# First FFN of a hybrid SSD/Hyena layer: gate and up products by seven block products, hidden values through DRAM, down product as a pass of its own

## The chip, the cores and the metric

The kernel runs on one core of a Trainium2 chip. The metric is the time of one execution on the device in microseconds (us), lower is better. The time before is the median of three runs.

## What is computed

One inference step of a layer over 1280 tokens: 1024 latent tokens (shift, scale and gate from `c`) and 256 context tokens (from `c_ctx`). The model width is 1024, the FFN width 2752, and all arithmetic is to float32 accuracy. Cut to what matters here:

```python
def swiglu(h, w_gate, w_up, w_down):
    return jnp.dot(jax.nn.silu(jnp.dot(h, w_gate)) * jnp.dot(h, w_up), w_down)

def trunk_layer(x, cond, ssd_init, n_rows, p):
    mod = jnp.dot(jax.nn.silu(cond), p['w_ada']) + p['b_ada']
    sh1, sc1, g1, sh2, sc2, g2, sh3, sc3, g3 = jnp.split(mod[:, None, :], N_MOD, axis=-1)
    h = modulate(rmsnorm(x, p['norm_ffn1']), sh1, sc1)
    x = x + 0.5 * g1 * swiglu(h, p['ffn1_w_gate'], p['ffn1_w_up'], p['ffn1_w_down'])
    h = modulate(rmsnorm(x, p['norm_mix']), sh2, sc2)
    mix, final_state = token_mix(h, ssd_init, n_rows, p)
    x = x + g2 * mix
    h = modulate(rmsnorm(x, p['norm_ffn2']), sh3, sc3)
    x = x + 0.5 * g3 * swiglu(h, p['ffn2_w_gate'], p['ffn2_w_up'], p['ffn2_w_down'])
    return x, final_state
```

A final RMSNorm follows. The change is in the first `swiglu` and in what stands directly before and behind it.

## The kernel before

**Precision.** Every float32 operand of a large product is split into a high part, rounded for TensorE, and a low part, the rest: `split` has a cast on ScalarE (line 137) and a subtraction on VectorE (138). `mm3` (lines 629 to 633) then issues three matmuls, high by high, high by low and low by high. A 128x128 weight block against a tile of tokens is so three matmuls, one of each of lines 631, 632 and 633.

**Stages.** In order of time: a front stage (`filters`: the Hyena filters and their spectra, with the first 16 adaLN units and the first norm woven in), the first FFN, the mixer, the output product, the second FFN with the final norm.

**First FFN before** (`ffn`, from line 647). The FFN width is 21 full units of 128 and a half unit of 64 (`NFULL` = 21). Tokens are in groups of 512, 512 and 256. Units go in slabs of two: gate and up of both units for all three groups (tile `pg`, 8 blocks of the model width each), then the down product of the slab (tile `pd`), which VectorE adds into x, which stays in SBUF (line 701). After each slab `hook` runs some of the 56 remaining adaLN units. The closing slab goes by a table (`PLAN1`), in which groups are finished in the order 2, 0, 1 and their norm for the mixer is woven into the rest.

**An adaLN unit** (`mod_unit`) is one 512 KB load (`wa`) and two multiply-and-sum instructions of 128x1024 on VectorE (`junk`, line 173), with a few very short ones.

**Second FFN before**, the scheme that the change copies. `products` (line 341) takes the tokens in two halves of 640 (`HT`; matmuls are 320 wide, `HB`) and the model width in two halves of 4 blocks. For each full unit gate and up weights are a 2x2 block matrix and tokens another, and seven block products (`P1` to `P7`) stand in for eight:

```python
"P1": (p("A11", "B11", "z", "pp1"), ...), "P6": (p("S2", "T2", "w", "pp6"), ...),
"P2": (p("A12", "B21", "z"), ...),        "P7": (p("S3", "T3", "x", "pp7"), ...),
"P5": (p("S1", "T1", "y", "pp5"), ...),   "P4": (p("A22", "T4", "x"), ...), "P3": (p("S4", "B22", "y"), ...)
```

One block product is 2 token strips x 4 blocks x 3 matmuls = 24 matmuls of 320 columns. `T1` to `T4` are differences of weight blocks (VectorE); `S1` to `S4` are sums of the modulated token halves, made once by `halves_s`: per k two operations on VectorE (514, 516) and two on GpSimd (515, 517), then `cut` splits each (S2's high parts are among the tiles `yp`, its low parts are `S2l`). The half unit 21 takes four plain products (`pt`). The list `ramp` of products that need no sums comes first (six items in the second FFN). The results leave PSUM by ScalarE copies and VectorE additions (`e1` to `e7`), and the hidden values go to DRAM. `strassen` (481) prepares weights four items ahead. Then `down_steps` (520) goes over the token groups one after the other: per step one unit's hidden values (`hraw`, split into `hs`) and its down weights (`wd`, split into `dh` and `dl`), two steps ahead, 8 x 3 matmuls into 8 PSUM banks; x is loaded again from DRAM and the eviction adds it. Weights of nine units are kept in split form after the first pass, the others are loaded and split again for each group.

**Order of work.** Each engine takes its instructions in the order in which a scheduler puts them for that engine when the kernel is built; semaphores are the only coupling. All loads here are issued by SyncE (SP), in order too. Tile pools with few buffers make a load wait for the last reader of the buffer that it fills.

Of the kernel before, what the change touches and what calls it, by code (L numbers as in the profile page):

```python
# [18 lines left out]
D = 1024  # L19
# [91 lines left out]
class Kern:  # L111
# [7 lines left out]
    def setup(self):  # L119
# [11 lines left out]
        self.wn = 0  # L131
        self.silu = None
# [176 lines left out]
    def rstd_half(self, x, tp, pp, ptag, dst):  # L309
# [13 lines left out]
        def mm():  # L323
            st["ps"] = pp.tile([128, 2, 512], F32, name="nps", tag=ptag)[:, :, :HB]
            for b in range(2):
                nc.tensor.matmul(st["ps"][:, b, :], self.ones, st["acc"][:, HB * b:HB * b + HB], start=True, stop=True)
# [14 lines left out]
    def products(self, wgu, hidd, S, wp, tt, ee, pp, raws, ramp, hook=None):  # L341
# [14 lines left out]
        def tsum(name, j, a, b):  # L356
            if (j, name) not in made:
                t = made[j, name] = tt.tile([128, 512], F32, name=name, tag=name)
                nc.vector.tensor_tensor(out=t, in0=a, in1=b, op=ALU.subtract)
            return made[j, name]  # L360
# [9 lines left out]
            "V2": lambda j: tsum("t2", j, half_raw(1, 1), half_raw(1, 0)),  # L370
        }

        def half_raw(half, k):
            if ("t", half, k) not in made:
                t = made["t", half, k] = tt.tile([128, 512], F32, name=f"wt{half}{k}", tag=("t1", "t3")[k])
                nc.sync.dma_start(t, wgu[2 * NFULL][:, 512 * k:512 * k + 512])
            return made["t", half, k]
# [30 lines left out]
        def pair(j):  # L408
# [27 lines left out]
            def e4():  # L436
                c = et("c21", "c21")
# [41 lines left out]
        return [(prep(j, c), f, e, load(j, c)) for j, (f, c, e) in seq]  # L479
# [47 lines left out]
    def down_steps(self, wdn, hidd, xsrc, mg, order, js, keep, at, each, pre, tick=None):  # L527
# [70 lines left out]
        def loadx(g, dm):  # L598
            g0, gw, _ = GROUPS[g]
            x[g, dm] = at(None)["x"].tile([128, 512], F32, name="xr", tag="x")[:, :gw]  # L600
# [168 lines left out]
    def win_zdt(self, h, zd, wz, rz, tp, pp, ptag):  # L769
        nc = self.nc  # L770
        w = [[self.wsplit(self.i["wz"][half, q], width=WUNIT, pool=wz, rp=rz) for q in range(2)] for half in range(2)]
# [424 lines left out]
    def filter_lat(self, o, hbig, w3, dl, ctn, caf, cb, tp, kp, pp, ptag):  # L1196
# [29 lines left out]
        def spec(bk):  # L1226
# [18 lines left out]
            def s3():  # L1245
                kk = kp.tile([128, T], F32, name="fk", tag="h")
                k = kk[:, 0:512]
                nc.scalar.copy(k, r["pz"])
                if bk == 0:
                    q = kk[64:65, 512:1024]  # L1250
# [338 lines left out]
    def build(self):  # L1589
# [13 lines left out]
        hp0 = sb("hp0")  # L1603
        h0 = self.hpool(hp0, "h", (0,))
        xp, hd, tp, modp = sb("xp", side="right"), sb("hd", 4, "right"), sb("tp", 2, "right"), sb("modp", side="right")
        nr = sb("nr", side="right")
        x = tiles(xp, "x")

        def load_x():
            for k in range(KD):  # L1610
                nc.sync.dma_start(x[k], i["xT"][k])
        mods = [(lambda u=u: self.mod_unit(u, modp)) for u in range(16)]
        np1 = sb("np1", 3, "right")
        r1 = []
# [3 lines left out]
        np1.release()  # L1618
        hp1, pp = sb("hp1"), psum("pp", 4)
        h = pair({**h0, **self.hpool(hp1, "h", (1, 2))})  # L1620
        self.wp = sb("wp", 6)
        self.wb = sb("wb", 4)
        fs = self.norm_items(x, 0, h, 2, TagPool(pp, "dn"), pp, "gu", tp)
# [355 lines left out]
```

## Time and profile before

| what | us |
|---|---|
| median of 3 runs (2673.14 to 2676.66) | 2673.55 |
| the profiled execution's own time | 2677.57 |
| its span in the trace | 2675.8 |
| TensorE (PE) busy | 2602.1 (97%) |
| VectorE (DVE) busy | 1519.8 (57%) |
| ScalarE (ACT) busy | 964.9 (36%) |
| GpSimd (POOL) busy | 16.6 (1%) |
| mean granted TensorE clock, share of full | 0.991 |

The profile is of one execution. PE's busy time is the union of its matmuls' records; records overlap, so the pace is read from start to start. A line number is a line of the kernel before. In the trace's rows a tile is named without its number (`pp1` is `pp`), a weight load is PEld, and "[4.03 <-ACT yp L137]" behind an instruction says that its engine sat idle for 4.03 us before it and which instruction ended that.

### The profile page before, as it was taken

How to read it: one execution, taken by the hardware profiler on the slowest of the kernel's cores; microseconds unless marked ns; L12 is line 12 of the kernel's file. 1: busy time of each engine (PE TensorE's matmuls, PEld its weight loads, DVE VectorE, ACT ScalarE, POOL GpSimd, SP SyncE). 2: the span in 40 equal slices, each digit the busy share in tenths (PEclk: the TensorE clock that was granted, in tenths of full speed). 3: DMA queues.
4: the chain of work that ended last, by engine and by line, in shares of the span. 5: the costliest groups of instructions: out<-in, count | busy, mean ns of one | idle time of the engine just before them, and what ended most of it. 6: DMA issues, size and time to landing. Idle time of an engine off the chain costs nothing.

```text
span 2675.8 us, 37129 instructions
## 1 busy us (share of the span) xinstructions
PE 2602.1 (97%) x14843; PEld 2268.5 (85%) x14843; DVE 1519.8 (57%) x2584; ACT 964.9 (36%) x1689; POOL 16.6 (1%) x15
## 2 busy tenths in 40 slices
PE   7999999999999999999999898997999999999998
PEld 3668888888888888798778787997999999988888
DVE  7677545655456336815885457569545545542445
ACT  4772111111111114623784676445222222232233
POOL 0000000000000000000000000002000000000000
PEclk9999999999999999999999999998999999999999
DMA  7433222222222112211224434631222222263334
GB/s 259 141 112 109 87 79 79 80 71 72 78 79 86 41 32 87 94 52 52 73 67 154 144 120 141 213 121 58 71 76 78 66 63 78 65 219 116 127 126 151
DMA packets 127184, 268.68 MB, mean 100 GB/s; under 512 B 14423, under 2 KB 50079, under 8 KB 126627
## 3 DMA queue, kind: packets, MB, share of 16 engines
q1 hardware_dynamic: 127011, 266.31, 31.2%
q8 instruction: 116, 1.90, 0.3%
q14 instruction: 57, 0.47, 0.1%
HBM read 211.53 MB, written 54.73 MB: 100 GB/s over the span
## 4 chain that ended last, share of the span: by engine, by line
PE 88%; DVE 5%; ACT 3%; DMA 2%; issue 1%; SPq 0%; POOL 0%; DVEq 0%; ACTq 0%; POOLq 0%
PE pg L631 7%; PE pg L633 7%; PE pg L632 7%; PE pd L631 7%; PE pd L633 7%; PE pd L632 7%; PE pp L632 6%; PE pp L633 6%; PE pp L631 6%; PE pc L631 3%; PE pc L632 3%; PE pc L633 3%; PE po L632 1%; PE po L633 1%; PE po L631 1%
## 5 line engine op out<-in xcount | busy, mean ns | idle before, releaser
L631 PE MATMUL pg<-hh,wh 128*128 128x512 f32 (+1 forms) x1032 | 366.2, 355 | 2.0 <-ACT wh L137 2.0
L633 PE MATMUL pg<-hh,wl 128*128 128x512 f32 (+1 forms) x1032 | 365.6, 355 | 0.0
L632 PE MATMUL pg<-hl,wh 128*128 128x512 f32 (+1 forms) x1032 | 365.4, 355 | 0.0
L631 PEld LDWEIGHTS pg<-hh,wh 128*128 128x128 f32 x1032 | 195.3, 189 | 30.4 <-ACT wh L137 3.3
L633 PEld LDWEIGHTS pg<-hh,wl 128*128 128x128 f32 x1032 | 195.4, 189 | 27.4 <-DVE wl L138 0.4
L632 PEld LDWEIGHTS pg<-hl,wh 128*128 128x128 f32 x1032 | 195.3, 189 | 27.1
L631 PE MATMUL pp<-yp,wT 128*128 128x320 f32 x672 | 209.6, 312 | 8.9 <-ACT yp L137 8.8
L633 PE MATMUL pp<-yp,wT 128*128 128x320 f32 x672 | 209.4, 312 | 0.0
L701 DVE SCALAR_TENSOR_TENSOR x<-pd,mod,x 128x512 f32<-128x512 f32 (+1 forms) x264 | 167.4, 657 | 51.1 <-PE pd L633 46.8
L173 DVE CUSTOM_DVE_ANT_0 junk<-wa,scb 128x1024 bf16<-128x1024 f32 x144 | 175.5, 1219 | 36.2 <-DMA wa<-wada 35.3
L138 DVE TENSOR_TENSOR wl<-wr,wh 128x1024 fp32r<-128x1024 f32 (+1 forms) x103 | 125.3, 1224 | 114.2 <-ACT wh L137 113.5
L631 PE MATMUL pd<-hh,wh 128*128 128x512 f32 (+1 forms) x504 | 182.1, 361 | 0.5 <-DVE x L701 0.5
L633 PE MATMUL pd<-hh,wl 128*128 128x512 f32 (+1 forms) x504 | 179.7, 357 | 0.0
L632 PE MATMUL pd<-hl,wh 128*128 128x512 f32 (+1 forms) x504 | 179.3, 356 | 0.0
L631 PE MATMUL pd<-hs,dh 128*128 128x512 f32 (+1 forms) x504 | 177.5, 355 | 1.0 <-DVE nm L220 0.8
L632 PE MATMUL pd<-hs,dh 128*128 128x512 f32 (+1 forms) x504 | 178.1, 354 | 0.1
L633 PE MATMUL pd<-hs,dl 128*128 128x512 f32 (+1 forms) x504 | 177.5, 354 | 0.0
L137 ACT CAST wh<-wr 128x1024 fp32r<-128x1024 f32 (+1 forms) x103 | 107.1, 1048 | 174.5 <-PE pd L632 52.9
L673 ACT ACTIVATE ft<-pg 128x512 f32<-128x512 f32 (+1 forms) x66 | 34.6, 524 | 354.9 <-PE pg L633 354.8
L631 PE MATMUL pc<-hh,wh 128*128 128x512 f32 (+1 forms) x432 | 154.8, 360 | 1.5 <-ACT hh L239 1.5
L631 PE MATMUL pp<-sh,wB 128*128 128x320 f32 x504 | 156.1, 310 | 0.0
L633 PE MATMUL pp<-sh,wB 128*128 128x320 f32 x504 | 155.6, 309 | 0.0
(381 smaller groups left out, 5819.8 us busy)
## 6 DMA issues: line engine op xcount, KB each, us to landing
wa<-wada SPq DMA_DIRECT2D x72, 512.0 KB, 3.6
wd<-wdn SPq DMA_DIRECT2D x45, 512.0 KB, 3.3
wr<-wgu SPq DMA_DIRECT2D x43, 512.0 KB, 3.5
wg<-wgu SPq DMA_DIRECT2D x42, 512.0 KB, 3.6
wr<-wdn SPq DMA_DIRECT2D x21, 512.0 KB, 3.5
hraw<-hidd SPq DMA_DIRECT2D x42, 256.0 KB, 2.6
wr<-wc SPq DMA_DIRECT2D x18, 512.0 KB, 3.6
kd<-fk SPq DMA_DIRECT2D x32, 256.0 KB, 2.4
```

What stands on the lines that cost most here:

```text
L137: nc.scalar.copy(hi, src)
L138: nc.vector.tensor_tensor(out=lo, in0=src, in1=hi.bitcast(F32), op=ALU.subtract)
L173: nc.vector.tensor_tensor_reduce(out=junk, in0=w, in1=self.scb[cond], scale=1.0, scalar=0.0, op0=ALU.mult, op1=ALU.add, accum_out=self.mod ...
L631: nc.tensor.matmul(ps, wh, rh, start=first, stop=False, **more)
L632: nc.tensor.matmul(ps, wh, rl, start=False, stop=False, **more)
L633: nc.tensor.matmul(ps, wl, rh, start=False, stop=last, **more)
L673: self.silu = nc.scalar.activation(t, pg, AF.Silu)
L701: nc.vector.scalar_tensor_tensor(out=x[dm][:, sl], in0=ps[dm], scalar=self.mod[:, mg, dm, cond:cond + 1], in1=x[dm][:, sl], op0=ALU.mult, ...
```

## The change

The first FFN takes the scheme of the second. In detail:

- `ffn` is no longer called. `products` and `down_steps` run for the first FFN as well, with hidden values in `hida`, token halves from a new input `xP` (x with each half's tokens side by side) and `ramp` of four items. Matmuls of 320 columns, 21 x 7 x 24 + 4 x 24 = 3624 of them, take the place of 3096 of 512 and 256; the down product keeps its number and widths.
- Front stage: `norms0` normalizes and modulates both halves (16 tiles, each two VectorE and two ScalarE instructions, of 512 and 128 columns) and splits half 0. Before, it was the norm of group 0 with its 8 modulated, split tiles and the root of group 1; the rest of the norm ran inside the first FFN.
- Down pass of the first FFN: groups in the order 0, 1, 2. Only units 2 to 5 keep their split weights, and these are given up at step 3 of the third pass, when the buffers of group 2's mixer input are made.
- adaLN units: one with each item of `B11` and `B21` from item 9 on (two in a unit's seven items, 40 in all), through a single buffer (`mw`), the next load issued behind the unit; 16 more in steps 1 to 16 of the first down pass, also through one buffer.
- Handover to the mixer: group 2's norm comes last, other order of the first mixer units.
- Shared helpers (so the second FFN too): `T1` is split right behind `T2` and not at its own product; `tt` is one tag of two buffers; tile `c21` comes from another pool; `rstd_half` writes two single PSUM banks and reads them by two instructions. `win_zdt` loses a raw buffer of its own; the filters' tile `fk` is 512 wide.

The core of the diff:

```diff
+    def mod_load(self, u, pool):
+        self.mraw[u] = pool.tile([128, D], F32, name=f"wa{u}", tag="wr")
+        self.nc.sync.dma_start(self.mraw[u], self.i["wada"][u])
+
     def mod_unit(self, u, pool):
...
-        w = self.raw(f"wa{u}")
-        nc.sync.dma_start(w, self.i["wada"][u])
+        if u not in self.mraw:
+            self.mod_load(u, self.rp)
+        w = self.mraw.pop(u)
...
@@ rstd_half @@
-            nc.vector.tensor_scalar(out=v2(m), in0=st["ps"], scalar1=1.0 / D, scalar2=EPS, op0=ALU.mult, op1=ALU.add)
+            for b, ps in enumerate(st["ps"]):
+                nc.vector.tensor_scalar(out=m[:, HB * b:HB * b + HB], in0=ps, scalar1=1.0 / D, scalar2=EPS, op0=ALU.mult,
+                                        op1=ALU.add)
...
@@ products @@
-                t = made[j, name] = tt.tile([128, 512], F32, name=name, tag=name)
+                t = made[j, name] = tt.tile([128, 512], F32, name=name, tag="t")
...
+        order = [(j, c) for j, (_, c, _) in seq]
+        for j in range(NFULL):
+            order.remove((j, "T1"))
+            order.insert(order.index((j, "T2")) + 1, (j, "T1"))
+        return [(prep(*order[n]), f, e, load(*order[n]), c) for n, (j, (f, c, e)) in enumerate(seq)]
...
@@ the program @@
-        self.filters(sb, psum, hd, lambda: self.mod_begin(modp), one(mods), lambda pp, ptag: one(
-            self.norm_items(x, 0, pair(h0), 0, np1, pp, ptag) +
-            self.rstd_items(x, 1, r1, np1, pp, ptag, dst=nr.tile([128, 512], F32, name="r1"))), load_x)
+        def norms0(pp, ptag):
+            banks = lambda: [pp.tile([128, 512], F32, name="nps", tag=ptag)[:, :HB] for _ in range(2)]
+
+            def mod(half, k):
+                self.modulate(xa[half][k], rr[half], 0, k)
+                if half == 0:
+                    self.split(xa[0][k], a1[0][k], a1[1][k])
+            out = []
+            for half in range(2):
+                out += self.rstd_half(xa[half], np1, banks, lambda half=half: rr[half])
+                out += [lambda half=half, k=k: mod(half, k) for k in range(KD)]
+            return one(out)
+        self.filters(sb, psum, hd, lambda: self.mod_begin(modp), one(mods), norms0, load_x)
...
+        sbp, mw = sb("sbp", 5, "right"), sb("mw", 1, "right")
+        sums, cut = self.halves_s(S, xa, xp, a1, yt, sbp)
+        items = self.products(i["wgu1"], hidd, S, self.wp, tt, ee, xp, pp, [self.rp] * 2,
+                              [(0, "P1"), (0, "P2"), (NFULL, None), (NFULL, None)])
...
+        def mods1(pool):
+            self.mod_unit(units.pop(0), modp)
+            if units:
+                self.mod_load(units[0], pool)
+
+        def more(s):
+            if s < 2:
+                for k in (2 * s, 2 * s + 1):
+                    sums(k)
+                    cut("S2", k)
+            elif s < 6:
+                for k in range(4):
+                    cut(("S3", "S1", "A22", "S4")[s - 2], k)
+            elif s > 8 and items[s][4] in ("B11", "B21"):
+                mods1(mw)
...
+        def tick(p, q):
+            if p and 2 <= q < 2 + KD:
+                norms[p - 1][KD - 1 + q]()
+            if p == 0 and q and units:
+                mods1(pl["mw"])
+            if p == 2 and q == 3:
+                pl["keep"].release()
+                ps = pl["h2"], pl["xg"], pl["np", 2] = sb("hp2"), sb("xg", 8), sb("xn", 4)
...
+        load, split, step, n = self.down_steps(i["wdn1"], hidd, i["xT"], 2, (0, 1, 2), [range(NFULL + 1), rest, rest],
+                                               range(2, 6), at, each, lambda p: norms[p - 1][KD](), tick)
+        self.strassen(items, 4, more, {len(items) - 1: prologue})
...
-        tail = self.ffn(i["wgu1"], i["wdn1"], h, x, 2, hd, tp, pp, after, hook, begin, (2, 0, 1), PLAN1, turn)
...
-        pipe([un[j][2] for j in range(3)])
-        run(tail[:KD])
-        pipe([un[0][0], un[1][0]])
-        run(tail[KD:KD + 1])
-        pipe([un[2][0]])
-        run(tail[KD + 1:])
+        pipe([un[0][0]])
+        run(norms[2][KD:KD + 1])
+        pipe([un[1][0], un[2][0]])
+        run(norms[2][KD + 1:])
+        pipe([un[j][1] for j in range(3)])
```

**Three places in the order of instructions.** The first is ScalarE at the end of the front stage. There `fut` and `fk` are the copies of the filters' spectra, `hh` is a modulated high part for the first FFN, `xa_117` to `xa_119` are modulated tiles of half 1. Before:

```order
165 L1248 COPY fk<-pfz 128x512
166 L1239 COPY fut<-pft 128x512
167 L192 ACTIVATE nr<-nm 128x512
168 L1248 COPY fk<-pfz 128x512
169 L193 ACTIVATE nr<-nr 128x512
170 L1248 COPY fk<-pfz 128x512
171 L137 CAST wh_1423<-wr_1421 128x1024
```

With the change:

```order
186 L347 ACTIVATE xa_117<-xa_117,mod 128x128
187 L1262 COPY fk<-pfz 128x512
188 L1254 COPY fut<-pft 128x512
189 L347 ACTIVATE xa_118<-xa_118,mod 128x512
190 L347 ACTIVATE xa_118<-xa_118,mod 128x128
191 L1262 COPY fk<-pfz 128x512
192 L1254 COPY fut<-pft 128x512
193 L347 ACTIVATE xa_119<-xa_119,mod 128x512
```

Between two spectra's copies there now stand two modulations of half 1; before, the last copies had only the reciprocal root between them.

The second is VectorE where the first FFN begins. Before, it made the weights' low parts (`wl`) and the modulated tokens of group 1:

```order
210 L138 TENSOR_TENSOR wl_1428<-wr_1427,wh_1429 128x1024
211 L237 SCALAR_TENSOR_TENSOR nt<-x_121,msc,r_374 128x512
212 L237 SCALAR_TENSOR_TENSOR nt<-x_122,msc,r_374 128x512
213 L237 SCALAR_TENSOR_TENSOR nt<-x_123,msc,r_374 128x512
214 L240 SCALAR_TENSOR_TENSOR hl_0_1391<-nt,mod,hh_0_1383 128x512
```

Now (`t` is a difference of weight blocks, `sf` and `xa` are sums of token halves, `S2l` a low part of S2, `wa` an adaLN row):

```order
246 L367 TENSOR_TENSOR t_1534<-wg_1_1528,wg_0_1513 128x512
247 L531 TENSOR_TENSOR xa_105<-sf_1481,xa_105 128x640
248 L367 TENSOR_TENSOR t_1536<-wg_1_1528,t_1534 128x512
249 L182 TENSOR_SCALAR mod<-mod,pkt 128x2
250 L179 ISA junk,mod<-wa_1933,scb_255 128x1024
251 L179 ISA mod 128x1
252 L139 TENSOR_TENSOR wT_0_1533<-t_1536,wT_0_1533 128x512
253 L139 TENSOR_TENSOR S2l_1571<-xa_105,sy_1465 128x640
254 L529 TENSOR_TENSOR sf_1482<-xa_114,xa_118 128x640
```

The sums stand between weight splits and halves of adaLN units; the modulations are all ahead of them.

The third is VectorE in the first down pass. Before, adaLN units stood in the first FFN between the splits of the hidden values (`hl`):

```order
365 L674 TENSOR_TENSOR ft<-ft,pg 128x512
366 L138 TENSOR_TENSOR hl_2139<-ft,hh_2138 128x512
367 L173 ISA junk,mod<-wa_2531,scb_248 128x1024
368 L173 ISA mod 128x1
```

Now a step's splits and one unit alternate:

```order
937 L139 TENSOR_TENSOR dl_7261<-wd_7215,dh_7262 128x1024
938 L139 TENSOR_TENSOR hs_7265<-hraw,hs_7265 128x512
939 L179 ISA junk,mod<-wa_7211,scb_255 128x1024
940 L179 ISA mod 128x1
941 L179 ISA junk,mod<-wa_7211,scb_258 128x1024
942 L179 ISA mod 128x1
943 L182 TENSOR_SCALAR mod<-mod,pkt 128x2
944 L139 TENSOR_TENSOR dl_7305<-wd_7259,dh_7306 128x1024
```

The splits for a later step (`dl_7305`) stand behind a unit whose row comes through the one buffer.

## Rows read from the trace of the kernel before

**Rows 1.** Page, part 4: the chain that ended last, shares of the span by engine.

```profile
PE 88%; DVE 5%; ACT 3%; DMA 2%; issue 1%; SPq 0%; POOL 0%; DVEq 0%; ACTq 0%; POOLq 0%
```

**Rows 2.** Busy time by windows; columns: window, length, engines (instructions), PEclk, DMA share, GB/s.

```profile
111.00:168.00 57.00, 52.89 (x260) 33.08 (x258) 34.70 (x58) 49.71 (x90) 0.00 (x0) 1.00 0.33 107
143.00:168.00 25.00, 23.22 (x98) 12.78 (x98) 11.14 (x17) 24.67 (x49) 0.00 (x0) 1.00 0.44 147
235.00:1030.00 795.00, 795.00 (x4165) 682.64 (x4163) 409.82 (x678) 119.41 (x178) 0.00 (x0) 1.00 0.23 72
1840.00:1845.00 5.00, 0.95 (x4) 0.55 (x3) 2.78 (x5) 3.93 (x7) 2.75 (x2) 0.50 0.37 102
1850.00:2275.00 425.00, 424.94 (x2884) 424.68 (x2882) 229.50 (x328) 108.11 (x174) 0.00 (x0) 1.00 0.24 72
2640.00:2654.00 14.00, 14.00 (x119) 14.00 (x118) 6.67 (x10) 5.98 (x9) 0.00 (x0) 1.00 0.64 207
```

**Rows 3.** PE by tile (pg, pd, pp): count, ns min/median/max, first and last start.

```profile
L631 PE MATMUL pg<-hh,wh x1032: 277/389/796, 169.1 to 1061.4; 128*128 128x512 f32 x127, 128*128 128x256 f32 x45
L694 PE MATMUL pd<-hs,wl x24: 278/392/402, 1015.9 to 1072.9; 128*128 128x512 f32 x16, 128*128 128x256 f32 x8
L631 PE MATMUL pp<-sh,wB x504: 304/309/556, 1805.4 to 2358.9; 128*128 128x320 f32 x168
L631 PE MATMUL pd<-hs,dh x504: 278/389/800, 2359.4 to 2659.9; 128*128 128x512 f32 x112, 128*128 128x256 f32 x56
L589 PE MATMUL pd<-hs,dl x24: 279/389/390, 2474.4 to 2662.0; 128*128 128x512 f32 x16, 128*128 128x256 f32 x8
```

**Rows 4.** Timeline of PE; start, duration. 27 steps lie between the first two, 26 between the last.

```profile
599.77 0.39 PE L631 MATMUL pg<-hh,wh 128*128 128x512 f32 x1
...
605.89 0.39 PE L631 MATMUL pg<-hh,wh 128*128 128x512 f32 x1
...
1999.69 0.31 PE L632 MATMUL pp<-S3l,wT 128*128 128x320 f32 x1
...
2003.52 0.31 PE L631 MATMUL pp<-yp,wT 128*128 128x320 f32 x1
```

**Rows 5.** Timeline of PE: the two longest idle times at the second FFN's start.

```profile
1834.76 0.64 PE L631 MATMUL pp<-yp,wT 128*128 128x320 f32 x1 [4.03 <-ACT yp L137]
...
1844.91 0.64 PE L631 MATMUL pp<-yp,wT 128*128 128x320 f32 x1 [4.05 <-ACT yp L137]
```

**Rows 6.** Groups at the second FFN's start, 1815 to 1850 us: busy us, mean ns, idle before.

```profile
L337 DVE SCALAR_TENSOR_TENSOR xa<-xa,msc,nr 128x512 f32<-128x512 f32 x8 | 11.2, 1396 | 0.0
...
L515 POOL TENSOR_TENSOR xa<-xa,xa 128x640 f32<-128x640 f32 x4 | 7.4, 1870 | 1825.5 <-DVE sf L514 1825.5
...
L516 DVE TENSOR_TENSOR xa<-sf,xa 128x640 f32<-128x640 f32 x4 | 4.5, 1152 | 1.4 <-POOL xa L515 1.4
...
L138 DVE TENSOR_TENSOR wT<-t,wT 128x512 fp32r<-128x512 f32 x4 | 2.7, 683 | 0.1
```

**Rows 7.** Groups on ACT: `hh` from 111 to 168.1 us, the others from 1690 to 1850 us.

```profile
L239 ACT ACTIVATE hh<-nt,mod 128x512 fp32r<-128x512 f32 x8 | 5.8, 721 | 0.2
...
L339 ACT ACTIVATE xa<-xa,mod 128x512 f32<-128x512 f32 x16 | 11.6, 723 | 5.4 <-DVE xa L337 5.4
...
L137 ACT CAST sh<-xa 128x640 fp32r<-128x640 f32 x12 | 8.4, 725 | 0.2
...
L339 ACT ACTIVATE xa<-xa,mod 128x128 f32<-128x128 f32 x16 | 6.3, 394 | 1.9 <-DVE xa L337 1.9
```

**Rows 8.** Page, parts 5 and 6: adaLN units; the last column is issue to landing, us.

```profile
L173 DVE CUSTOM_DVE_ANT_0 junk<-wa,scb 128x1024 bf16<-128x1024 f32 x144 | 175.5, 1219 | 36.2 <-DMA wa<-wada 35.3
...
wa<-wada SPq DMA_DIRECT2D x72, 512.0 KB, 3.6
```

**Rows 9.** Timeline of PE: idle times between the first FFN and the mixer.

```profile
1094.63 1.12 PE L217 MATMUL nps<-nacc,ones 128*128 128x512 f32 x2 [1.45 <-DVE nacc L212]
...
1102.50 0.98 PE L631 MATMUL pc<-hh,wh 128*128 128x512 f32 x3 [1.48 <-ACT hh L239]
```

More of the change, by code (lines that the diff above doesn't have):

```diff
@@ new lines, in build, with late, tile, each @@
+        pl, norms, h = {}, {}, [{}, {}]
+        at = lambda s: {"raw": (self.rp, D, "wr"), "hid": (self.wp, "w")} if s is not None and s < 2 else pl
+        def late(g):
+            class Late:
+                def tile(_, shape, dtype, name, tag):
+                    return pl["psum"].tile(shape, dtype, name=name, tag="b" if g == 2 else "dn")
+            return Late()
+        def each(g, dm, x):
+            g0, gw, _ = GROUPS[g]
+            nc.sync.dma_start(xd[dm][:, g0:g0 + gw], x[g, dm])
+            if dm == 0:
+                norms[g] = self.norm_items(lambda k: x[g, k], 1, h, g, pl["np", g], late(g), "dn")
+            else:
+                norms[g][dm - 1]()
+            if dm == KD - 1:
+                norms[g][dm]()
@@ new lines, in tick @@
+        def tick(p, q):
[6 more added lines that the diff above has]
+                ps = pl["h2"], pl["xg"], pl["np", 2] = sb("hp2"), sb("xg", 8), sb("xn", 4)
+                for n in range(2):
+                    h[n][2] = [ps[0].tile([128, 256], F32R, name=f"h2{n}{k}") for k in range(KD)]
+        rest = [2, 3, 4, 5, 0, 1, *range(6, NFULL + 1)]
@@ new lines, in build @@
+        hp0, hp1, kp = sb("hp0"), sb("hp1"), sb("kp1", 8)
+        mw, hd, xr, npp = sb("mw1", 1, "right"), sb("hd1", 3, "right"), sb("xr1", 12, "right"), sb("npp", 5, "right")
+        pd = psum("pd1", 8)
+        for m in range(2):
+            h[m][0] = [hp0.tile([128, 512], F32R, name=f"h0{m}{k}") for k in range(KD)]
+            h[m][1] = [hp1.tile([128, 512], F32R, name=f"h1{m}{k}") for k in range(KD)]
+        pl.update({"raw": (hd, 512, "r"), "hid": (hd, "h"), "keep": kp, "x": lambda g: pl["xg"] if g == 2 else xr,
+                   "psum": pd, "mw": mw, ("np", 0): npp, ("np", 1): npp})
@@ L1662, in build @@
+        load(2)
+        pre = {}
+        for s in range(n):
+            if s + 3 < n:
+                load(s + 3)
+            if s + 2 < n:
+                split(s + 2)
+            else:
+                j = (4, 0)[s + 2 - n]
+                pre[j] = self.wsplit(i["wc"][j])
+            step(s)
+        pre[1] = self.wsplit(i["wc"][1])
+        for p in (npp, xr, hd, mw, modp, pd):
             p.release()
         sp, pm = sb("sp", side="right"), psum("pm", 4)
-        late.pool = pm
+        pl["psum"] = pm
@@ L1732, in build, with wide @@
         pl = {}
+        def wide():
+            t = pp.tile([128, 2, 512], F32, name="nps", tag="g")
+            return [t[:, b, :HB] for b in range(2)]
         r0 = np2.tile([128, HT], F32, name="nr", tag="r", bufs=1)
-        n0, n1 = self.rstd_half(xa[0], np2, pp, "g", lambda: r0), self.rstd_half(xa[1], np2, pp, "g", lambda: new_r1())
+        n0, n1 = self.rstd_half(xa[0], np2, wide, lambda: r0), self.rstd_half(xa[1], np2, wide, lambda: new_r1())
         def new_r1():
@@ L1767, in more @@
                     pl["cut"](("S3", "S1", "A22", "S4")[s - 3], k)
-        items = self.products(i["wgu2"], hidd, S, self.wp, tt, ee, pp, raws, ramp)
+        items = self.products(i["wgu2"], hidd, S, self.wp, tt, ee, xp, pp, raws, ramp)
         def at(s):
```

124 lines of the change are left out of this document (53 added, 71 removed).

## Prediction

> **What bounds the kernel now.** I read the chain that ended last first [rows 1]: 88% of the span is PE. So I looked for the stretches in which PE never rests and for those in which it does, by the windows view [rows 2]. From 235 to 1030 us, inside the first FFN, PE is busy 795.00 of 795 us at full granted clock, DVE about half and ACT 15%; from 1850 to 2275, in the second FFN's products, 424.94 of 425. Such a stretch gets shorter only by less matmul time. At the end of the front stage it is different: from 143 to 168 us ACT is busy 24.67 of 25 us, and PE runs at the pace of ACT's copies. At the start of the second FFN PE waits: the timeline shows idle times of 4.03 and 4.05 us before products that need S2 [rows 5], and from 1840 to 1845 us PE did 0.95 us of work at a granted clock of 0.50, its lower level [rows 2].
>
> The views by tile give the stages' borders [rows 3]. The first FFN runs from 169.1 (first `pg`) to 1072.9 (last `pd`): 903.8 us. The second runs from 1805.4 (first `pp`) over 2359.4 (first `pd`) to 2662.0: 554.0 us of products and 302.6 of down pass, 856.6 together. It is the same computation in the scheme that the first FFN is to take, so it is this kernel's own measurement of the change's core.
>
> The timeline gives the pace [rows 4]. 27 steps of 512 columns took 6.12 us, 0.2267 each; 26 steps of 320 took 3.83, 0.1473 each. A line through both gives 0.413 ns per column and a fixed 15 ns, so 0.121 us at 256 columns.
>
> **The products.** Removed: 1032 matmuls of each of three lines, two thirds 512 wide and a third 256 wide, 3 x (688 x 0.2267 + 344 x 0.121) = 593 us. Added: 3624 x 0.1473 = 534. The down product keeps its matmuls. Ideally that is -59 us. Seven products for eight would be -74; the narrower matmuls' fixed part takes 15 of it. I take the second FFN's stage as a whole instead, 856.6 for 903.8: **-47.2**. It holds 554.0 - 534 = 20 us of loss in its products, nearly all at their start, and 3 to 4 in its down pass.
>
> A rule of the Trainium skill speaks against narrowing (TensorE: Matmul & The Clock Gate, Back-to-back issue gap): in a sustained stream of weight loads and matmuls it gives some 81 ns a matmul at 128 columns and 131 at 512. Between them that is about 106 at 320 and 97 at 256, an estimate from that page, and by it the products would go from 371 to 384 us, slower by 13. The trace does not agree: 227 and 147 ns.
>
> **The start of the products.** In the second FFN VectorE does the modulations (8 instructions of 1.396 us beside GpSimd's [rows 6], and 8 short ones) in the same queue as the sums. The change has them all ahead of the first product, in the front stage, as the order shows. From the first weight split to the last `S2l` VectorE's queue now holds about nine 512-wide instructions (0.683), three halves of adaLN units (1.219 [rows 8]) and twelve 640-wide ones, which beside GpSimd's take up to 1.152 [rows 6]: 6.1 + 3.7 + 13.8, near 23 us. The four items of the ramp are 4 x 24 x 0.147 = 14.1 us of PE work, and three quarters of the first S2 product can run before the last `S2l`, 2.7 more. That leaves some 6 us of waiting, and 3 or 4 at the lower clock behind it, against 20: **-10** (0 to -15; nothing if the shorter ramp eats it all).
>
> The skill says of this place (SBUF, State Buffer, Who interferes with whom) that a VectorE operation with two SBUF inputs and a GpSimd operation that reads SBUF exclude each other for the whole instruction. By it the sixteen sums would simply add up. The trace shows less for most, 1.152 for 640 columns beside GpSimd's 1.870.
>
> **The front stage.** Added on ACT: 16 modulations of 0.723 and 16 of 0.394, 17.9 us, and 8 casts of 0.725, 5.8. Gone: 8 `hh` of 0.721, 5.8 [rows 7]. So 18 us more on the engine that sets the pace here. From 111 to 168 us ACT has 57 - 49.7 = 7.3 us free [rows 2]. The rest delays the first product: **+10**. At best some of it moves further ahead, +5; at worst the free time isn't usable, +15. VectorE gains about as much work, but is busy only 34.7 of the 57.
>
> **adaLN units among the products.** 40 units of 2 x 1.219 us on VectorE, two in each 24.8 us (seven items): its share goes from 229.5/425, 54%, to 74%. It works in order, so an addition that frees PSUM may come up to 2.4 us late, against a product's 3.54. The nearest row is the first FFN before, which ran the same units beside DVE at 52% and lost nothing [rows 2]; at the other end 0.5 us a unit would be 20. I take **+4**, near the row.
>
> **adaLN units in the down pass.** One buffer: two `junk`s, then the next load, 3.6 us to landing [rows 8], 6.1 to 6.3 a unit against 24 x 0.2267 = 5.44 a step. Over 16 steps VectorE falls 11 to 14 us behind, with `dl` and `hs` of later steps queued behind the waiting unit. They are made two steps ahead, 10.9 us. So 0 to +5, **+3**.
>
> **Fewer weights kept.** Group 2 now loads 18 units' weights at 2.88 us a step. The nearest row is the end of the second FFN's down pass with loads in a row: PE 14.00 of 14.00 us, DMA 0.64 [rows 2]. Group 1's norm stands beside them on VectorE and its high end is +5: **+2**.
>
> **Handover.** Before, PE waited 1.45 and 1.48 us here [rows 9]; with group 2 alone at the end and units of other groups between, **-2** (-3 to +2).
>
> **Nothing** for the hidden values' way through DRAM (the second FFN has it at 0.24 of the DMA engines; were the queue late, the first steps of the down pass would show it, 2 us each), for `T1` moved and for `c21`, `tt`, `fq` and `rstd_half` (VectorE and ACT have room; without it 0 to +3), and for `win_zdt`'s lost buffer (0 to +2).
>
> **Sum:** -47.2 - 10 + 10 + 4 + 3 + 2 - 2 = -40.2, from the profiled 2677.6 to 2637.4. The median of the runs is 4.0 below the profiled execution, which gives 2633; I say 2634.
>
> **Rivals.** (a) *Stalls vanish*: S2 is ready when the ramp ends (-15), front +5, units hidden, handover -3: -60, 2613. For it speaks that the first FFN before hid such units; against it VectorE's 23 us at the start. Chance 0.14.
> (b) *Half eaten*: front +15, start -3, units +12, down pass +5 and +5, handover 0: -13, 2660. For it speaks ACT at 24.67 of 25; it covers 2646 to 2668. Chance 0.27.
> (c) *Slower*: VectorE, at 74% and in order, makes PSUM come free late at every adaLN unit. At 1.24 us for each of 40, 50 in place of 4, the kernel is 0.2% slower; at the full 2.44 us it is 2727. Against it, the 795 us without a PE wait; for it, that two additions of a unit's products (`e7`, `e5`) must be done within one product's 3.54 us. Chance 0.04, with another 0.04 for coming out level on the way there.
> (d) *Narrow matmuls cost more than the seven products save*: the sum holds as long as a matmul of 320 columns starts every 0.1473 us; at 0.1584 (0.1473 + 40.2 / 3624) the kernel is level, at 0.1599 slower by 0.2%, and at 0.1636 (593 / 3624, no gain in the products) it would be 2693. The second FFN shows 0.1473, and 424.94 busy of 425 us. Chance 0.01. The skill's spacing above is of this sort.
> That the change does not do what it says is out: the order has the 3624 matmuls.
>
> **How the numbers follow.** My forecast has 0.50, by itself 2622 to 2646 (each term's ends, not all at once). What a measurement can tell here is 0.2%, 5.3 us: faster is below 2668, slower above 2679. Faster: 0.50 + 0.14 + 0.27 = 0.91; same 0.04; slower 0.04 + 0.01. The range of 8 in 10 leaves out half of (a) below and, above, the worse half of (b) with what is slower: 2613 to 2658.
>
> **What would show it.** Products near 545 us from first to last `pp` and a down pass near 307; the first `pp` near 179 rather than 169 us, with ACT busy before it; one PE wait of a few microseconds on `S2l` or its high part, with the granted clock at its lower level right behind it; `junk` waiting for `wa` in the first down pass without PE gaps over 5 us in all. Wrong would be: PE waits for `e5` or `e7` all through the products (c), a first `pp` past 185 (b), or a stage of the second FFN that changed by more than 3 us.

## The result, and the profile after

| | before | with the change |
|---|---|---|
| median of the runs, us | 2674.33 (4 runs, one more than at the prediction) | 2647.39 (4 runs, 2641.27 to 2648.02) |
| ratio | | 0.9893, 95% interval 0.9876 to 0.9910 |
| profiled execution, us | 2677.57 | 2648.02 |
| its span, us | 2675.8 | 2646.2 |

The kernel is 1.1% faster, 27 us; 40 were forecast. The time, 2647.4, lies within the range (2613 to 2658), 13 us above the forecast of 2634. The spans of the two profiled executions differ by 29.6 us, and the rest of this section goes by them.

The page of the kernel with the change, part 1 and part 4 (compare [rows 1]):

```profile
PE 2551.4 (96%) x15373; PEld 2294.0 (87%) x15373; DVE 1610.0 (61%) x2668; ACT 1069.1 (40%) x1848; POOL 34.4 (1%) x23
...
PE 80%; DVE 8%; DMA 5%; ACT 4%; issue 2%; SPq 0%; DVEq 0%; ACTq 0%
```

PE is busy 51 us less than before (2602.1), but the span lost only 29.6: PE now rests some 21 us more. In the chain DVE, DMA and ACT together went from 10% to 17%.

Its PE by tile, first and last starts; the first row is the first FFN's products, the other two its down pass (compare [rows 3]):

```profile
L646 PE MATMUL pp<-ah,wB x336: 305/309/469, 181.5 to 716.0; 128*128 128x320 f32 x168
...
L646 PE MATMUL pd<-hs,dh x504: 277/392/796, 730.6 to 1040.7; 128*128 128x512 f32 x112, 128*128 128x256 f32 x56
...
L604 PE MATMUL pd<-hs,dl x24: 276/392/399, 849.3 to 1042.9; 128*128 128x512 f32 x16, 128*128 128x256 f32 x8
```

So the first product starts at 181.5 (before 169.1), the products take 549.1 us, the down pass 312.3, the stage 861.4 for 903.8. The second FFN is what it was, 553.9 and 302.7 us in both kernels (554.0 and 302.6 by the rounded starts of [rows 3]). Between the last `pd` of the first FFN and the first `pp` of the second lie 732.9 us, before 732.5.

| stage | forecast change | measured |
|---|---|---|
| front, to the first product | +10 | +12.4 |
| products, against the second FFN's 554.0 | -6 (start -10, units +4) | -4.9 |
| down pass, against the second FFN's 302.6 | +5 | +9.7 |
| the second FFN's 856.6 for the first's 903.8 | -47.2 | -47.2 by construction |
| from there to the second FFN | -2 | +0.4 |
| sum | -40.2 | -29.6 |

The same windows view as in [rows 2], of the kernel with the change: front's end, products, first and second token group of the down pass.

```profile
140.00:181.00 41.00, 32.60 (x148) 18.84 (x146) 21.48 (x37) 37.28 (x73) 0.00 (x0) 1.00 0.27 91
...
235.00:730.00 495.00, 495.00 (x3377) 495.00 (x3377) 350.86 (x567) 127.75 (x200) 0.00 (x0) 1.00 0.36 114
730.00:850.00 120.00, 119.36 (x513) 95.77 (x513) 80.55 (x128) 34.10 (x44) 0.00 (x0) 1.00 0.75 244
850.00:967.00 117.00, 117.00 (x500) 93.46 (x499) 56.64 (x75) 44.08 (x60) 0.00 (x0) 1.00 0.47 153
```

ACT is busy 37.28 of 41 us ahead of the products, and PE rests 8.4 of them. From 235 us on PE never rests in the products, with VectorE at 71%: there the units cost nothing. In the down pass PE seems full too, and this reading deceived me. A busy PE says only that records overlap. In the second group 500 matmuls fill 117.00 us, 0.234 each, where [rows 4] had 0.2267 for the same width.

From start to start, 27 steps of 512 columns each. The first group of the down pass with the change:

```profile
799.63 0.39 PE L647 MATMUL pd<-hs,dh 128*128 128x512 f32 x1
...
805.93 0.39 PE L647 MATMUL pd<-hs,dh 128*128 128x512 f32 x1
```

6.30 us, 0.2333 a step. And the kernel before, in a place that I had not looked at, the first FFN's down product:

```profile
311.01 0.39 PE L631 MATMUL pd<-hh,wh 128*128 128x512 f32 x1
...
317.30 0.40 PE L631 MATMUL pd<-hh,wh 128*128 128x512 f32 x1
```

6.29 us. It ran at 0.233 there as well, while its gate and up product ran at 0.2267. The rows from which I took the pace were of the gate product. The first two groups have some 1040 matmuls of this width, and at all of them the difference would be 6.9 us. The kernel before paid that, and the change pays nearly all of it: its first two steps still run at the fast pace, as shown next.

### The profile page after: what moved, and what is told of

The parts are those of the page before. It is cut to its first block, busy times and chain, and to the rows that moved or that the text cites. A ratio compares the mean times of both kernels' runs of the same rounds, so it can differ in the third digit from the quotient of the medians.

```text
span 2646.2 us, 39082 instructions
## 1 busy us (share of the span) xinstructions
PE 2551.4 (96%) x15373; PEld 2294.0 (87%) x15373; DVE 1610.0 (61%) x2668; ACT 1069.1 (40%) x1848; POOL 34.4 (1%) x23
## 4 chain that ended last, share of the span: by engine, by line
PE 80%; DVE 8%; DMA 5%; ACT 4%; issue 2%; SPq 0%; DVEq 0%; ACTq 0%
PE pp L647 13%; PE pp L648 13%; PE pp L646 13%; PE pd L647 5%; PE pd L646 5%; PE pd L648 5%; PE pc L646 3%; PE pc L647 3%; PE pc L648 3%; DMA wa<-wada 2%; DMA wd<-wdn 2%; DVE junk L179 1%; PE po L648 1%; PE po L647 1%; PE po L646 1%
## 5 line engine op out<-in xcount | busy, mean ns | idle before, releaser
L647 PE MATMUL pd<-hs,dh 128*128 128x512 f32 (+1 forms) x1008 | 358.2, 356 | 0.6 <-DVE hs L139 0.4
L648 PE MATMUL pd<-hs,dl 128*128 128x512 f32 (+1 forms) x1008 | 357.3, 356 | 1.0 <-DVE dl L139 1.0
L646 PE MATMUL pd<-hs,dh 128*128 128x512 f32 (+1 forms) x1008 | 356.2, 357 | 2.1 <-DVE nm L226 1.6
L139 DVE TENSOR_TENSOR dl<-wd,dh 128x1024 fp32r<-128x1024 f32 x106 | 129.5, 1223 | 199.2 <-ACT dh L138 193.3
L646 PEld LDWEIGHTS pd<-hs,dh 128*128 128x128 f32 x1008 | 188.7, 188 | 34.8 <-DVE nm L226 3.8
L647 PEld LDWEIGHTS pd<-hs,dh 128*128 128x128 f32 x1008 | 190.2, 189 | 30.1 <-DVE hs L139 1.4
L648 PEld LDWEIGHTS pd<-hs,dl 128*128 128x128 f32 x1008 | 189.7, 188 | 29.5 <-DVE dl L139 1.6
L646 PE MATMUL pp<-sy,wT 128*128 128x320 f32 x672 | 209.0, 311 | 2.5 <-ACT sy L138 2.5
L648 PE MATMUL pp<-sy,wT 128*128 128x320 f32 x672 | 208.8, 311 | 0.0
L139 DVE TENSOR_TENSOR wT<-t,wT 128x512 fp32r<-128x512 f32 x168 | 115.3, 687 | 73.7 <-ACT wT L138 73.2
L646 PE MATMUL pc<-h,wh 128*128 128x512 f32 (+1 forms) x432 | 156.2, 362 | 1.5 <-DVE xr L609 1.5
L647 PE MATMUL pc<-h,wh 128*128 128x512 f32 (+1 forms) x432 | 154.2, 357 | 0.0
L648 PE MATMUL pc<-h,wl 128*128 128x512 f32 (+1 forms) x432 | 154.0, 357 | 0.0
L646 PEld LDWEIGHTS pp<-yp,wT 128*128 128x128 f32 x672 | 127.3, 190 | 11.2 <-ACT yp L138 10.4
```

The source lines that it names most:

```text
L139: nc.vector.tensor_tensor(out=lo, in0=src, in1=hi.bitcast(F32), op=ALU.subtract)
L646: nc.tensor.matmul(ps, wh, rh, start=first, stop=False, **more)
L647: nc.tensor.matmul(ps, wh, rl, start=False, stop=False, **more)
L648: nc.tensor.matmul(ps, wl, rh, start=False, stop=last, **more)
```

## The experiments

Ten kernels ran beside the kernel before. Differences are against the change's median, 2647.39 us, if nothing else is said. Runs of one kernel spread over 3 to 7 us, and the kernel before, which ran in each of the four sets of runs, had medians from 2674.3 to 2676.5. So for effects of a few microseconds the stages of the profiled executions, read from first and last starts, carry the verdict and the medians only go with them. Each kernel has one profile, and a stage that a run does not touch is itself some 1 us longer or shorter from one to the next; the mixer with the output product varies more, from 728 to 733 us.

### Where the hidden values lie

The pace does not go with the traffic beside it: the first group has adaLN units and 244 GB/s, the second none and 153, and both show 0.233. What the two first down products have in common against the second FFN's is where the moving operand lies. In the built programs the buffers of the first FFN's hidden values (`hd`, `hd1`) begin 32 bytes past a multiple of 64, those of the second (`hd2`) at a multiple of 128.

The changed kernel holds a first test of this. The hidden values of the first two steps of its down pass lie in another pool (`wp`), at multiples of 128. These lines are the first matmuls of its second, third and fourth step, 24 matmuls from one to the next:

```profile
736.55 0.39 PE L646 MATMUL pd<-hs,dh 128*128 128x512 f32 x1
...
741.99 0.40 PE L646 MATMUL pd<-hs,dh 128*128 128x512 f32 x1
...
747.60 0.39 PE L646 MATMUL pd<-hs,dh 128*128 128x512 f32 x1
```

The second step takes 5.44 us, 0.2267 a matmul, and the third, the first one from `hd1`, 5.61, or 0.2338; later steps are at 0.2333. The first run moves these buffers by 32 bytes; `pad` is a tile that only takes up room.

```diff
-        mw, hd, xr, npp = sb("mw1", 1, "right"), sb("hd1", 3, "right"), sb("xr1", 12, "right"), sb("npp", 5, "right")
+        mw, pad = sb("mw1", 1, "right"), sb("pad", 1, "right")
+        nc.vector.memset(pad.tile([128, 8], F32, name="pad32"), 0.0)
+        hd, xr, npp = sb("hd1", 3, "right"), sb("xr1", 12, "right"), sb("npp", 5, "right")
```

> The buffers of the first down pass's hidden values (hd1) are moved by 32 bytes per partition, so that they begin at a multiple of 64 bytes as the second FFN's do; nothing else changes. Theory (place of the moving operand): the 512-wide matmuls of the first two token groups start every 0.2267 us instead of 0.2333, and the down pass gets shorter by about 1040 x 0.0066 = 6.9 us, the kernel too. Rival (the loads and VectorE's work beside the pass slow the matmuls): pace stays at 0.2333, time within 1 us of the changed kernel.

Measured: 2641.37 us, 6.0 less; down pass 306.8 for 312.3. The pace, 27 steps:

```profile
899.93 0.39 PE L647 MATMUL pd<-hs,dh 128*128 128x512 f32 x1
...
906.11 0.39 PE L647 MATMUL pd<-hs,dh 128*128 128x512 f32 x1
```

6.18 us, 0.2289: two thirds of the way. The buffers are now at a multiple of 64, not of 128. So once more:

```diff
-        nc.vector.memset(pad.tile([128, 8], F32, name="pad32"), 0.0)
+        nc.vector.memset(pad.tile([128, 24], F32, name="pad32"), 0.0)
```

> As the run with 32 bytes, but the hidden values' buffers of the first down pass are moved by 96 bytes, to a multiple of 128 as the second FFN's are. With 32 bytes (a multiple of 64) the 512-wide matmuls of that pass went from 0.2333 to 0.2289 us apart, not to the second FFN's 0.2267. Theory (the place of the moving operand sets all of it, by steps of its alignment): 0.2267, down pass some 2 us shorter than with 32 bytes, 304 to 305 us, kernel near 2639. Rival (the rest comes from something else in the stage, as loads or the weights' place): 0.2289 again, 306 to 307 us.

```profile
900.01 0.39 PE L646 MATMUL pd<-hs,dh 128*128 128x512 f32 x1
...
906.13 0.39 PE L646 MATMUL pd<-hs,dh 128*128 128x512 f32 x1
```

6.12 us, 0.2267, as in the second FFN. So the pace of the 512-wide matmuls follows the place of the moving operand: 0.2333 us where the tile begins 32 bytes past a multiple of 64, 0.2289 at a multiple of 64 that is none of 128, 0.2267 at a multiple of 128. But the down pass took 308.1 us and the kernel 2641.05, no better than with 32 bytes: I missed that. The timeline of PE in the first group shows one reason:

```profile
823.55 0.50 PE L647 MATMUL pd<-hs,dh 128*128 128x512 f32 x1 [0.24 <-DVE hs L139]
829.69 0.50 PE L647 MATMUL pd<-hs,dh 128*128 128x512 f32 x1 [0.38 <-DVE hs L139]
842.62 0.50 PE L647 MATMUL pd<-hs,dh 128*128 128x512 f32 x1 [1.34 <-DVE hs L139]
```

PE now waits for `hs`, which stands on VectorE behind an adaLN unit. Such a unit takes some 6.2 us through its one buffer; a step has 24 matmuls, 5.44 us at the fast pace and 5.60 at the slow one. The slow matmuls had hidden most of this: the change has one such wait, of 0.43 us. A run below takes the units away, and the waits go with them.

A second, smaller reason is in the third group, whose matmuls are 256 wide. 27 steps with 32 bytes, then with 96:

```profile
994.77 0.28 PE L646 MATMUL pd<-hs,dh 128*128 128x256 f32 x1
...
997.95 0.28 PE L646 MATMUL pd<-hs,dh 128*128 128x256 f32 x1
```

```profile
997.80 0.28 PE L646 MATMUL pd<-hs,dh 128*128 128x256 f32 x1
...
1001.04 0.28 PE L646 MATMUL pd<-hs,dh 128*128 128x256 f32 x1
```

That is 3.18 us against 3.24, 0.1178 a step against 0.1200, and the change itself has 0.1198. Over 520 matmuls the place at 64 is worth 1.1 us here: what is best at 512 columns is not best at 256.

The kernel before with the same 96 bytes, and with its (second FFN's) token sums on VectorE, which the next experiment is on:

```diff
-        xp, hd, tp, modp = sb("xp", side="right"), sb("hd", 4, "right"), sb("tp", 2, "right"), sb("modp", side="right")
+        xp, pad = sb("xp", side="right"), sb("pad", 1, "right")
+        nc.vector.memset(pad.tile([128, 24], F32, name="pad32"), 0.0)
+        hd, tp, modp = sb("hd", 4, "right"), sb("tp", 2, "right"), sb("modp", side="right")
```

> The kernel before with two of the repairs: its first FFN's hidden values at a multiple of 128 bytes, and the second FFN's token sums on VectorE. Theory (the kernel before already paid 0.2333 for its first down product's 1008 wide matmuls, so the prediction's template counted a gain that was no part of the change's scheme): 6 to 7 us from the first FFN and 4 to 5 from the second, 11 in all, about 2663. Rival (the slow pace is of the new pass alone): only the 4 to 5 us of the second FFN, about 2670.

Measured: 2664.42 us against 2675.43, ratio 0.9958 (0.9943 to 0.9973). Its first FFN runs from 171.4 to 1067.8, 896.4 for 903.8, and its wide down matmuls, 27 steps:

```profile
311.65 0.40 PE L631 MATMUL pd<-hh,wh 128*128 128x512 f32 x1
...
317.80 0.39 PE L631 MATMUL pd<-hh,wh 128*128 128x512 f32 x1
```

6.15 us, 0.2278 here and 0.2270 on the mean of 64 rounds of three. The slow pace is not the change's; it belongs to the buffers' place in either kernel. Why its first FFN begins 2.3 us later than before stays open. With both repairs on both sides the change would probably be worth more than 27 us, but no run has the change with just these two. The first kernel of the last experiment has them and two more, and lies 39.9 us under this one; less the 5.5 and 2.2 us that the other two gave singly, that leaves some 32 us, an estimate.

### The start of the products: GpSimd beside VectorE

In the change PE's waits for S2 in the first FFN are these (timeline of PE; at the second FFN's start before there were two of over 4 us, [rows 5]):

```profile
202.84 0.63 PE L646 MATMUL pp<-sy,wT 128*128 128x320 f32 x1 [2.49 <-ACT sy L138]
...
206.30 0.64 PE L647 MATMUL pp<-S2l,wT 128*128 128x320 f32 x1 [2.82 <-DVE S2l L139]
...
209.11 0.63 PE L647 MATMUL pp<-S2l,wT 128*128 128x320 f32 x1 [1.64 <-DVE S2l L139]
...
211.80 0.64 PE L647 MATMUL pp<-S2l,wT 128*128 128x320 f32 x1 [1.52 <-DVE S2l L139]
```

VectorE and then GpSimd in the same stretch, timeline:

```profile
199.93 2.16 DVE L529 TENSOR_TENSOR sf<-xa,xa 128x640 f32<-128x640 f32 x1
202.01 2.16 DVE L531 TENSOR_TENSOR xa<-sf,xa 128x640 f32<-128x640 f32 x1
204.09 2.15 DVE L139 TENSOR_TENSOR S2l<-xa,sy 128x640 fp32r<-128x640 f32 x1
206.16 2.15 DVE L531 TENSOR_TENSOR xa<-sf,xa 128x640 f32<-128x640 f32 x1
208.24 0.81 DVE L139 TENSOR_TENSOR S2l<-xa,sy 128x640 fp32r<-128x640 f32 x1
```

```profile
201.36 2.12 POOL L532 TENSOR_TENSOR xa<-xa,xa 128x640 f32<-128x640 f32 x1
203.45 2.11 POOL L530 TENSOR_TENSOR xa<-xa,xa 128x640 f32<-128x640 f32 x1
205.52 2.12 POOL L532 TENSOR_TENSOR xa<-xa,xa 128x640 f32<-128x640 f32 x1
```

An instruction of 640 columns takes 0.81 us, or 2.15 when GpSimd has one of its own: VectorE's end then follows GpSimd's within 0.7 us, one pair after the other. So semaphores are not all that couples these two engines here. My price, 1.152 [rows 6], was the mean of the two kinds: that row's four took 0.81, 2.16, 0.81 and 0.83 us. From the first weight split at 181.5 to the end of the last `S2l` at 211.7 VectorE took 30 us, where the prediction counted 23. The Trainium skill (SBUF — State Buffer, Who interferes with whom) says that a VectorE instruction with two SBUF inputs and a GpSimd one that reads SBUF take turns by an exclusive lock; I had read the mean as evidence against it, and the single durations, 0.81 and 2.15 us, agree with it.

The waits cost more than their own length, as the granted clock (0.50, in the third column from the right) fell to its lower level behind them:

```profile
205.00:210.00 5.00, 2.06 (x6) 1.53 (x6) 5.00 (x4) 2.05 (x3) 4.24 (x3) 0.50 0.00 0
210.00:215.00 5.00, 3.48 (x14) 3.20 (x13) 4.97 (x7) 3.50 (x6) 0.46 (x1) 0.50 0.14 33
```

```diff
-            nc.gpsimd.tensor_tensor(out=a21[k], in0=a11[k], in1=a21[k], op=ALU.subtract)
+            nc.vector.tensor_tensor(out=a21[k], in0=a11[k], in1=a21[k], op=ALU.subtract)
...
-            nc.gpsimd.tensor_tensor(out=a12[k], in0=a12[k], in1=a11[k], op=ALU.subtract)
+            nc.vector.tensor_tensor(out=a12[k], in0=a12[k], in1=a11[k], op=ALU.subtract)
```

> GpSimd's two subtractions per k of the token sums run on VectorE, in both FFNs. Theory (in the first FFN's start VectorE's 640-wide instructions take 2.15 us instead of 0.81 whenever GpSimd has one, about 8 x 1.3 us lost against 8 x 0.81 added): the waits for S2 of the first FFN (9.8 us in four) shrink by 4 to 8 us, likewise in the second FFN; kernel shorter by 6 to 14 us. Rival (VectorE's queue is the bound and GpSimd takes work off it): 16 instructions of 0.81 more, later by 3 to 6 us in each FFN.

Measured: 2634.14 us, 13.3 less. Groups on VectorE from 181 to 212 us (busy us, mean ns):

```profile
L531 DVE TENSOR_TENSOR xa<-sf,xa 128x640 f32<-128x640 f32 x4 | 3.3, 820 | 0.0
L529 DVE TENSOR_TENSOR sf<-xa,xa 128x640 f32<-128x640 f32 x4 | 3.3, 820 | 0.0
L530 DVE TENSOR_TENSOR xa<-xa,xa 128x640 f32<-128x640 f32 x4 | 3.3, 819 | 0.0
L139 DVE TENSOR_TENSOR S2l<-xa,sy 128x640 fp32r<-128x640 f32 x4 | 3.3, 817 | 0.0
```

All at 0.82. VectorE has eight instructions more, 6.6 us, and yet the last `S2l` ends at 207.2 us and not at 211.7. The granted clock is 0.50 from 205 to 210 us and already 0.83 from 210 to 215. The products take 543.5 and 549.5 us for 549.1 and 553.9: 5.5 and 4.3 won. Another 4.3 of the profiled difference lie in the untouched mixer and output product, which took 728 to 733 us across these runs; that part I don't count as an effect. So 10 us have a place, inside the theory's 6 to 14.

### The front stage

```diff
-                self.modulate(xa[half][k], rr[half], 0, k)
+                self.modulate(xa[half][k], rr[half], 0, k, half == 1)
...
+            if dve:
+                nc.vector.tensor_scalar(out=x[:, cs], in0=x[:, cs], scalar1=b, scalar2=None, op0=ALU.add)
+            else:
+                nc.scalar.activation(x[:, cs], x[:, cs], AF.Identity, bias=b)
```

> The shift of half 1's modulated tiles is added by VectorE and not by ScalarE (16 instructions), all else as in the change. Theory (ScalarE paces the end of the front stage): 8 x (0.72 + 0.39) = 8.9 us leave ScalarE, the first product starts 5 to 9 us earlier than 181.5, and the kernel is shorter by that. Rival (VectorE or the chain of the norm paces it, or the weights' arrival): first product within 2 us of 181.5, kernel unchanged or slower by up to 3 us.

Measured: 2641.84 us, 5.5 less; the first product starts at 175.8. The window up to it:

```profile
140.00:175.80 35.80, 30.68 (x148) 18.71 (x147) 24.62 (x49) 30.85 (x57) 0.00 (x0) 1.00 0.32 106
```

ACT is busy 30.85 us where it was 37.28 and PE rests 5.1 us for 8.4. In the change the longest of PE's waits here were for ScalarE's copies (view of waits, 140 to 181 us: total, times, longest):

```profile
PE pfz L1258 <- ACT fut L1254: 6.1, 8, 1.8
```

So ScalarE's added work set the end of the front stage: of the 8.9 us taken off it two thirds came back, 5.7. The products behind were no later for VectorE's 16 instructions more (549.5).

### adaLN units

```diff
-        units = list(range(16, 72))
-        self.mod_load(units[0], mw)
+        units = []
```

> The 56 adaLN units that ran among the products and in the first down pass are left out, their loads too; their values are a constant 0.5, so the outputs are not the reference's. Theory (the units are covered by PE's work and only their three halves at the start are in VectorE's way): products 1 to 4 us shorter, down pass shorter by under 1.5, pace of the 512-wide matmuls still 0.2333. Rival (the prediction's terms, +4 among the products and +3 in the down pass, and a slower pace through the loads' traffic): 7 us or more, with the pace back at 0.2267 in the first token group.

Measured: 2645.02 us (two runs), products 547.0 (2.1 less), down pass 311.3 (1.0 less), with the first group's 512-wide matmuls at 0.2333 on the average of 80 us. So the units cost 3 us at most, not the 7 of the forecast; the 1.0 of the down pass is no more than that stage varies by itself (311.1 in the run with the sums, which leaves it alone). The loads of the units have no part in the pace. In the down pass the units are cheap only beside slow matmuls, as the run with 96 bytes showed. Hence the next, the change with the 96 bytes and all units among the products:

```diff
-            elif s > 8 and items[s][4] in ("B11", "B21"):
+            elif s > 8 and items[s][4] in ("B11", "B21", "T4") and units:
                 mods1(mw)
```

> The change with hidden values at a multiple of 128 bytes (as the run with 96 bytes) and all 56 adaLN units among the products, three in a unit's seven items instead of two, none in the down pass. With the faster pace a step is 5.44 us, and with the units beside it the first token group had waits of 1.50, 0.54 and 0.39 us on hs; at 0.2333 a step was 5.60 and there was one of 0.59. Theory (a unit through one buffer takes about 6.2 us, more than a step of 5.44, so the queue falls behind): without units these waits go, down pass 304 to 305 us after 308.1; the products keep 495 busy of 495 us with VectorE near 79%, 549 us. Rival (VectorE at 79% makes PSUM free late): products 552 to 560 us, no gain.

Measured: 2638.46 us, 8.9 less than the change and 2.6 less than with 96 bytes alone; down pass 305.0, which is 3.1 less than with 96 bytes alone and without waits for `hs` in the first group; products 549.2 for the change's 549.1. The window in the products:

```profile
235.00:700.00 465.00, 465.00 (x3172) 464.99 (x3171) 374.39 (x633) 121.00 (x191) 0.00 (x0) 1.00 0.43 133
```

PE never rests with VectorE at 80.5%. Rival (c) of the prediction, that evictions come late at every unit, has no trace here, not even with half as many units again.

### Weights kept

```diff
-        rest = [2, 3, 4, 5, 0, 1, *range(6, NFULL + 1)]
+        rest = [2, 3, 4, 5, 6, 0, 1, *range(7, NFULL + 1)]
```

(and `kp1` of 10 buffers, `range(2, 7)`, released one step later)

> Five units instead of four keep their split weights in the first FFN's down pass; 17 instead of 18 loads in the second and third pass. Theory (with two raw buffers a load, cast and subtraction take 6.1 us for two steps of 2.88, so the third pass falls behind and PE waits about 3 us in its last steps): one step without a load wins back 2.9 us, the waits at the end (0.92 us and smaller ones) go, kernel shorter by 2 to 4 us. Rival (the end waits come from the mixer's weights' loads in the queue): unchanged within 1 us.

Measured: 2645.21 us, 2.2 less; down pass 309.4 for 312.3, and no wait of PE is left in its last 40 us, where the change had one of 0.76 for `dl` and smaller ones. The profiled pair agrees with the theory (2.9 us); the medians alone, whose runs spread over 5 us, would not prove it.

### All repairs together

The edits are those above: 96 bytes, sums, front, five units.

> The change with four repairs: hidden values at a multiple of 128 bytes, all token sums on VectorE, half 1's shifts on VectorE in the front stage, five units kept. Singly they gave 6.0 (32 bytes), 13.3, 5.5 and 2.2 us. If they add up: about 2620, first product near 176, products 543, down pass 301. If the front's VectorE work or the sums meet at the start of the products (rival): 2624 to 2630, with first waits for S2 longer than with the sums alone.

Measured: 2624.57 us, ratio to before 0.9807 (0.9792 to 0.9822). First product 176.2, products 543.8, down pass 306.8: the stage terms add up but for the down pass, where PE again waits for `hs` behind the units. With all units among the products:

> The four repairs together with all adaLN units among the products. The four alone gave 2624.6, with waits of 0.37 to 0.54 us on hs at four steps of the first token group and a down pass of 306.75 us. Theory: down pass 302 to 304, products 543 to 544, kernel 2620 to 2623. Rival (more units on VectorE at the products' start, where it is the bound): products 1 to 3 us longer, kernel 2623 to 2626.

Measured: 2621.73 us (five runs), ratio 0.9802 (0.9789 to 0.9815). Products 544.8 (1.1 longer), down pass 303.4 (3.3 shorter). Its down pass by tile, first and last start:

```profile
L650 PE MATMUL pd<-hs,dh x504: 277/389/799, 721.1 to 1021.6; 128*128 128x512 f32 x112, 128*128 128x256 f32 x56
...
L608 PE MATMUL pd<-hs,dl x24: 279/389/389, 836.1 to 1024.6; 128*128 128x512 f32 x16, 128*128 128x256 f32 x8
```

From the first product to the last `pd` are now 848.3 us, 8 less than the second FFN's 856.6 that I had as template. It is the fastest of all, 25.7 us under the change and 43 under the kernel before with two of the repairs (2664.42). By 2.8 us it is ahead of the version before it, which is no more than their runs spread; the stages show the gain and the medians don't contradict it.

## Why the prediction was right, and where it was not

**The core term, the direction and the range** were right. The products' pace in the new place is 495.00 / 3377 = 0.1466 us, against the 0.1473 of the forecast, and PE does not rest in them from 235 us on. That is far from the 0.1584 at which rival (d), narrow matmuls that cost more than the seven products save, would have left the kernel level.

**"It is this kernel's own measurement of the change's core"** is the step that failed most. It was true of the products and not of the down pass. Two stages that run the same instructions differ in where their tiles lie: 0.2333 for 0.2267 us over the 992 wide matmuls behind the first two steps is 6.5 us of the 9.7 by which the pass exceeds its template. So not all of the -47.2 was the scheme's: the kernel before with its first FFN's buffers moved takes 896.4 us for it, and against that the template's 856.6 gains 39.8. The traces of before held it; I read the pace at one tile (`pg`) and took it for the other (`pd`) too.

**The start, -10**: -4.9 with the units, -7.0 without them. The wait was found where it was said to be, on S2, with GpSimd's and VectorE's instructions one behind the other; the price of one beside GpSimd's was 2.15 us and not 1.152. The four waits of 8.5 us in all stand against the forecast's 6, and the lower clock came behind them as forecast, from about 205 to 215 us.

**The front, +10**: +12.4. The mechanism, ScalarE, was right and confirmed by taking work away. Its busy time up to the first product rose by 15.7 us (113.1 to 128.8), less than the 18 counted, and less of its free 7.3 us could be used: from 111 us to the first product it is still idle for 4.6.

**Units among products, +4, and in the down pass, +3**: 2.1 and at most 1.0. The second was right about the mechanism (units of 6.2 us against steps of 5.44) and mostly hidden by a step of 5.60; with fast matmuls the waits came, and taking the units out gave 3.1 us, the size of the forecast.

**Fewer weights kept, +2**: 2.9 us came back with one unit more, and in the last run, with five units kept, fast matmuls and no units beside it, the pass is 0.7 us over the second FFN's. So the term is 2.9 and at most 0.7 more, a little above the forecast.

**Handover, -2**: +0.4, nothing that these runs can tell from zero.

**From the profile to the median**: I took 4.0 us off, as before's profiled execution stood above its median. The change's stood 0.6 above. That is the other 3 us of the miss.

Of the rivals none came true as a whole; the outcome lies just inside the band given to (b), but not by its causes: its largest excess, +12 for the units, was +2, its front (+15) and start (-3) were missed by 2.6 and 4 us, and the slow step was in no case of mine. That the range held is in part luck, as nothing in it allowed for the slow step.

What stays open: how the matmul's step depends on the address beyond the three places tried, why 256 columns prefer another place than 512, and the 3 to 5 us by which the untouched mixer varies between these kernels.

## What to carry to other kernels

A stage of the same kernel is a good template for a new one, but compare the pace from start to start for each tile, since a busy PE at full clock can hide 3%. Try tiles that PE streams in 512-wide matmuls at multiples of 128 bytes in a partition; it cost one small padding tile here, and the last part of it paid only once nothing else held the steps up. Before work is given to GpSimd beside a loaded VectorE, look at single durations and not at a mean: here handing it back to VectorE made VectorE finish earlier.

## What the runs showed of the hardware that was not expected

A float32-rounded matmul of 512 columns started every 0.2267 us when the streamed tile began at a multiple of 128 bytes, 0.2289 at 64 past one and 0.2333 at 96 past one. At 256 columns it was 0.1200, 0.1178 and 0.1198 in the same three places. Those of 320 columns, whose tiles lie in part 96 past such a multiple too, kept 0.1466. Two-input VectorE instructions of 128x640 took 0.81 us alone and 2.15 beside GpSimd's, whose own took 2.1. And a repair gave nothing by itself, the 96 bytes instead of 32: it uncovered the next limit in the same steps, and the narrower matmuls lost what they had won.
